# Both parts of h side by side in one tile: 512 columns at once against the high part of the weights

## Chip, cores and metric

The kernel runs on one core of one Trainium2 chip. The time is that of one execution on the device, in microseconds (us); smaller is better. The engines are TensorE (PE; its weight loads are listed apart as PEld), VectorE (DVE), ScalarE (ACT), GpSimd (POOL) and SyncE (SP, which issues the loads).

## What is computed

One encoder block on 256 tokens of 2048 channels, in float32: a normalisation, one wide input projection, two branches (latent attention, and a bidirectional RWKV-7 recurrence over 16 heads of 64), gates, a merge and an output projection.

```python
h = rms_norm(x, g_pre)                       # 256 x 2048
proj = h @ w_in                              # 2048 x 10688
mla_in, rwkv_in, z_mla, z_rwkv, gate_mla, gate_rwkv = split(proj)
y_mla  = attention(norm(q_a) @ wq_b, norm(kv_a) @ wkv_b, k_rope)
y_rwkv = groupnorm(rwkv7_bidir_scan(r, w, k, v, kk, a)) + bonus
u_mla  = (y_mla  * silu(z_mla))  @ w_br_mla
u_rwkv = (y_rwkv * silu(z_rwkv)) @ w_br_rwkv
out = (sigmoid(gate_mla) * u_mla + sigmoid(gate_rwkv) * u_rwkv) @ w_out
x = x + rms_norm(out, g_post)
```

## The kernel before, in words

**Products in three parts.** Every float32 factor is split into a high part in the faster format float32r and a low part, the rest. A product is the sum of high times high, high times low and low times high. `hhi` and `hlo` are the two parts of h, transposed: 16 blocks (k) of 128 channels by 256 tokens. The weights come in chunks of 128x1024 (`raw`): ACT casts a chunk to its high part (`whi`, L321) and DVE subtracts to get the low part (`wlo`, L324); this pair is called a split. Three chunks can be in flight.

**In-tasks.** The input projection is cut into tasks of 256 output channels (`in_task`, `cm_task`): for each of 16 k and each of two blocks of 128 channels there are three matmuls with 256 columns, L390 (whi, hhi), L391 (whi, hlo) and L392 (wlo, hhi). Both blocks add up in one PSUM bank, 256 columns each. There are 40 in-tasks: 12 for k, r, v of the recurrence (`rwkv_tasks`), 8 for z, 8 for the gates of the attention branch, 4 low-rank ones, and 8 for the gates of the RWKV branch (`gate_rwkv_task`). The first, narrow part of the projection (`LORA`) has tasks of its own. When a task's matmuls are done, its `end` reads the bank: `mix` (k, r, v), `ev_z`, a Tanh (gates) or a copy (low rank).

**Banks.** PSUM has eight banks of 512 columns: three (`DB`) hold the sums of tasks, five (`MB`) serve everything else.

**The recurrence** runs for four groups Q of four heads one after the other (`chunks_of`). Each has a *gram* stage (L791 and L799 on PE, evicted by DVE), a *solve* of small triangular systems (DVE alone: transposes L812 and L813, 60 small dependent operations, transposes L840, L842 and L844; then 32x32 matmuls L854 and L856 with copies at L861), and four *steps* along time, in each of which L886/L906/L908, a copy, L917, a copy, and L935/L938 follow on each other. After group 3 come `wkv_task` (its first matmul is L1073), `wq_task` with the attention heads, the branch products and the output projection (L1328 to L1330).

**Order.** Nothing is scheduled at run time: a planner (`Streams`) lets about twenty generators ask for an engine with a cost in us (`yield ("P", cost)`), and always takes the one that can start first, with ranks for ties; instructions are emitted in that order, engine by engine. The in-tasks' matmuls have the lowest rank on PE and fill what the recurrence leaves. So a changed cost, bank or operation can move instructions anywhere. An engine works its list strictly in order.

Of the kernel before, what the change touches and what calls it, by code (L numbers as in the profile page):

```python
# [15 lines left out]
S = 256  # L16
# [27 lines left out]
class Streams:  # L44
# [6 lines left out]
    def __init__(self):  # L51
        self.free = dict.fromkeys("PADGS", 0.0)
        self.live = []
        self.used = dict.fromkeys("PADGS", 0.0)
        self.table = None

# [20 lines left out]
    def run(self, until=None):  # L77
        while self.live and not (until and until()):
# [30 lines left out]
            if len(s[3]) > 3 and s[3][3] != self.table:  # L109
# [26 lines left out]
def cD(n):  # L136
    return 0.08 + 1.04e-3 * n
# [11 lines left out]
def encoder_block_kernel(  # L149
# [52 lines left out]
    hhi, hlo = sb([128, KT, S], "hhi", dt=F32R), sb([128, KT, S], "hlo", dt=F32R)  # L202
# [5 lines left out]
    MB = Free(pps.tile([128, 512], F32, tag=f"m{i}", bufs=1, name=f"m{i}") for i in range(5))  # L208
    DB = Free(pps.tile([128, 512], F32, tag=f"d{i}", bufs=1, name=f"d{i}") for i in range(3))
# [155 lines left out]
    def cm_task(src, nk, xhi, xlo, mt, wd, end, kc=4, load_fn=None, ready=None, kready=None, k_first=0,  # L365
                begin=None, pairs=None, first_alone=False):

        parts = []
        nb = (len(mt) + 1) // 2
# [3 lines left out]
        for i, k0 in enumerate(k0s):  # L373
# [23 lines left out]
        def take():  # L397
            b = []
            for _ in range(nb):
                b.append((yield from DB.take()))  # L400
            return b

        add_task(parts, begin or take, end, ready)
# [56 lines left out]
    def ev_second(b):  # L460
        yield ("W", lambda: len(have.get("part", ())) == 2)
        for p, m, t, B in zip(b, (96, 128), have["part"], (DB, MB)):
            yield ("D", cD(512))
            tt(w2d(t)[0:m], w2d(t)[0:m], p2(p)[0:m], ALU.add)
            B.give(p)
# [48 lines left out]
    def ev_z(b, o):  # L514

        z = p2(b[0])
        t = yield from W.take()
        yield ("A", cA(512), None, "exp")
        act.activation(w2d(t), z, AF.Tanh, scale=0.5)
        yield ("D", cD(512))  # L520
        stt(o, w2d(t), 1.0, z, ALU.add, ALU.mult)
        W.give(t)
        DB.give(*b)
# [8 lines left out]
    def gate_mla_task(g):  # L532
        def end(b):
            yield ("A", cA(512), None, "exp")
            act.activation(m16[:, 2 * g:2 * g + 2], p2(b[0]), AF.Tanh, scale=0.5)
            DB.give(*b)
        in_task(GM0 + 256 * g, end)

    def low_rank_task(c0, key):
        def end(b):  # L540
            t = yield from W.take(KEEP)
            yield ("A", cA(512))
            act.copy(w2d(t), p2(b[0]))
            DB.give(*b)
# [30 lines left out]
    def head_sums(v, m):  # L575
# [3 lines left out]
        yield ("P", 0.44)  # L579
# [1068 lines left out]
```

## Time and profile before

| | |
|---|---|
| median of 3 runs | 885.38 us (884.04 to 886.46) |
| the profiled execution | 883.63 us |
| its span, first to last instruction | 881.9 us |
| PE busy | 851.0 us, 97% |
| DVE busy | 660.1 us, 75% |
| ACT busy | 501.0 us, 57% |
| mean granted clock of TensorE | 0.984 of 2.4 GHz |

How to read it: a matmul's duration in the trace reaches from its start to a modelled end, and the next one starts long before that end. So the busy share of PE says little; what a matmul costs is the distance from one start to the next. Idle time of an engine is put down to the instruction that released it.

### The profile page before, as it was taken

Reading aid. Unit: us, or ns where it says so; the run is one execution under the profiler, and the core shown is the slowest. Engines: PE = TensorE matmul, PEld = TensorE weight load, DVE = VectorE, ACT = ScalarE, POOL = GpSimd, SP = SyncE. Lnnn points to the kernel's source line nnn. Section 1 sums busy time; section 2 is a strip of 40 time slices with the busy share of each in tenths; the row PEclk is TensorE's granted clock in tenths of the full one; section 3 lists DMA queues with packets and bytes.
Section 4 is the critical chain, followed back from the end, with each engine's and each line's share of the span. In section 5 each row is a group of like instructions: output and inputs, shape, how many; then the busy total and the mean of one; then the engine's idle time right before and its main releaser. Section 6 shows DMA issues by size and latency. Waiting matters only on the chain.

```text
span 881.9 us, 19393 instructions
## 1 busy us (share of the span) xinstructions
PE 851.0 (97%) x8112; PEld 814.6 (92%) x8112; DVE 660.1 (75%) x1082; ACT 501.0 (57%) x797; POOL 30.8 (3%) x66
## 2 busy tenths in 40 slices
PE   8999999999999999999999997979999999999996
PEld 8999999899999999999899896879999999998884
DVE  5878898867988867998868988566868556775554
ACT  6688554478444478554478543656857433444442
POOL 4110000000000000000001000000000000000000
PEclk9999999999999999999999999879999999999999
DMA  9566546534746534646525365125545675655563
GB/s 283 167 176 182 165 123 193 164 84 113 194 136 192 165 84 121 192 134 189 161 63 147 97 192 167 32 69 171 168 115 144 206 277 186 191 178 198 195 196 117
DMA packets 123528, 139.41 MB, mean 158 GB/s; under 512 B 6704, under 2 KB 110512, under 8 KB 123056
## 3 DMA queue, kind: packets, MB, share of 16 engines
q1 hardware_dynamic: 121664, 135.16, 51.9%
q0 software_dynamic: 768, 1.57, 0.6%
q8 instruction: 63, 1.03, 0.5%
q10 hardware_dynamic: 1008, 1.44, 0.5%
q14 instruction: 25, 0.20, 0.1%
HBM read 136.05 MB, written 2.10 MB: 157 GB/s over the span
## 4 chain that ended last, share of the span: by engine, by line
PE 88%; DVE 6%; ACT 3%; DMA 1%; issue 1%; POOL 0%; SPq 0%; DVEq 0%; ACTq 0%
PE d L390 19%; PE d L391 18%; PE d L392 18%; PE m L1329 2%; PE m L1330 2%; PE m L1328 2%; PE m L392 2%; PE m L391 2%; PE m L390 2%; PE m L791 2%; DVE wlo L324 2%; PE d L1329 1%; PE d L1330 1%; PE d L1328 1%; PE m L917 1%
## 5 line engine op out<-in xcount | busy, mean ns | idle before, releaser
L321 ACT CAST whi<-raw 128x1024 fp32r<-128x1024 f32 (+3 forms) x252 | 253.1, 1006 | 255.9 <-PE d L391 147.0
L324 DVE TENSOR_TENSOR wlo<-raw,whi 128x1024 fp32r<-128x1024 f32 (+3 forms) x250 | 292.3, 1170 | 121.2 <-ACT whi L321 119.3
L390 PE MATMUL d<-hhi,whi 128*128 128x256 f32 (+1 forms) x1264 | 366.4, 290 | 3.1 <-ACT u L1265 1.9
L392 PE MATMUL d<-hhi,wlo 128*128 128x256 f32 (+1 forms) x1264 | 358.5, 284 | 0.0
L391 PE MATMUL d<-hlo,whi 128*128 128x256 f32 (+1 forms) x1264 | 358.3, 283 | 0.1
L390 PEld LDWEIGHTS d<-hhi,whi 128*128 128x128 f32 (+1 forms) x1264 | 241.5, 191 | 7.6 <-ACT u L1265 2.1
L391 PEld LDWEIGHTS d<-hlo,whi 128*128 128x128 f32 (+1 forms) x1264 | 241.9, 191 | 0.4 <-DVE hlo L188 0.3
L392 PEld LDWEIGHTS d<-hhi,wlo 128*128 128x128 f32 (+1 forms) x1264 | 241.8, 191 | 0.3 <-DVE wlo L324 0.2
L185 DVE TENSOR_TENSOR work<-work,work 128x512 f32<-128x512 f32 (+5 forms) x64 | 38.9, 613 | 6.7 <-ACT work L429 4.5
L185 DVE TENSOR_TENSOR u<-u,tmp 128x30 f32<-128x30 f32 (+7 forms) x120 | 29.9, 250 | 3.1
L185 DVE TENSOR_TENSOR tmp<-u 128x30 f32<-128x30 f32 (+7 forms) x120 | 29.9, 249 | 3.0
L390 PE MATMUL d<-b,whi 128*128 128x256 f32 x96 | 27.1, 282 | 0.0
L392 PE MATMUL d<-b,wlo 128*128 128x256 f32 x96 | 27.1, 282 | 0.0
L392 PE MATMUL d<-ar,wlo 128*128 128x256 f32 x96 | 26.9, 281 | 0.0
L391 PE MATMUL d<-ar,whi 128*128 128x256 f32 x96 | 26.9, 280 | 0.0
L391 PE MATMUL d<-work,whi 128*128 128x256 f32 x96 | 26.9, 280 | 0.0
L390 PE MATMUL d<-ar,whi 128*128 128x256 f32 x96 | 26.9, 280 | 0.0
L1328 PE MATMUL m<-whi,hhi 128*128 128x512 f32 x60 | 23.3, 389 | 0.0
L1329 PE MATMUL m<-wlo,hhi 128*128 128x512 f32 x60 | 23.3, 389 | 0.0
L1330 PE MATMUL m<-whi,hlo 128*128 128x512 f32 x60 | 23.3, 389 | 0.0
L390 PE MATMUL m<-hhi,whi 128*128 128x256 f32 x80 | 23.2, 290 | 0.0
L392 PE MATMUL m<-hhi,wlo 128*128 128x256 f32 x80 | 22.6, 282 | 0.0
(335 smaller groups left out, 1536.9 us busy)
## 6 DMA issues: line engine op xcount, KB each, us to landing
raw<-in_w_in_dram SPq DMA_DIRECT2D x160, 512.0 KB, 3.9
raw<-in_w_out_dram SPq DMA_DIRECT2D x32, 512.0 KB, 3.6
raw<-in_w_br_mla_dram SPq DMA_DIRECT2D x16, 512.0 KB, 3.6
raw<-in_w_br_rwkv_dram SPq DMA_DIRECT2D x16, 512.0 KB, 3.4
raw<-in_mla_wkv_b_dram SPq DMA_DIRECT2D x8, 512.0 KB, 3.6
raw<-in_mla_wq_b_dram SPq DMA_DIRECT2D x8, 384.0 KB, 3.3
raw<-in_w_in_dram SPq DMA_DIRECT2D x7, 384.0 KB, 5.4
g<-in_x_dram SPq DMA_DIRECT2D x2, 1024.0 KB, 7.4
```

The costliest lines, as they stand in the source:

```text
L185: dve.tensor_tensor(out=o, in0=a, in1=b, op=op)
L321: act.copy(dst(c.hi), src(raw))
L324: eng.tensor_tensor(out=dst(c.lo), in0=src(raw), in1=dst(c.hi).bitcast(F32), op=ALU.subtract)
L390: pe.matmul(o, hi[:, c:c + m], xhi(k), start=k == k_first and i % 2 == 0, stop=False)
L391: pe.matmul(o, hi[:, c:c + m], xlo(k), start=False, stop=False)
L392: pe.matmul(o, lo[:, c:c + m], xhi(k), start=False, stop=last)
L791: pe.matmul(m[:, q * 128:q * 128 + 128], z.kb[R64[h], d, j, q], z.ar[d][R64[h], j, q], start=q == 0, stop=q == 3)
L917: pe.matmul(pu[R64[i], a], G[Hs, st, q, 0:64], rhs[Hs, st % 2, st // 2], start=a == 0, stop=a == 3)
L1328: pe.matmul(banks[t], hhi[:, k, T], hi, start=k == 0, stop=False)
L1329: pe.matmul(banks[t], hhi[:, k, T], lo, start=False, stop=False)
L1330: pe.matmul(banks[t], hlo[:, k, T], hi, start=False, stop=k == KT - 1)
```

## The change

`hhi` and `hlo` become the halves of one tile `hh`, so that for each k one matmul with 512 columns multiplies the high part of the weights with both parts of h, and one with 256 columns adds the low part of the weights times `hhi` to the first half. A block of 128 channels then needs a PSUM bank of its own (first half: whi·hhi + wlo·hhi; second half: whi·hlo), an in-task two banks, and `DB` has four, `MB` four. A new function `total` adds the halves at the end of a task: two ACT copies of 128x256 out of PSUM, two DVE additions of 128x256. It is used by 32 of the 40 in-tasks; the 8 of `gate_rwkv_task`, the `LORA` tasks and all later products keep their three matmuls (L409 to L411 of the changed file). In the same edit many costs given to the planner are set anew, and PE's switches between tile shapes cost 0.2 in it. What it computes is the same.

```diff
-    hhi, hlo = sb([128, KT, S], "hhi", dt=F32R), sb([128, KT, S], "hlo", dt=F32R)
+    hh = sb([128, 2, KT, S], "hh", dt=F32R)
+    hhi, hlo = hh[:, 0], hh[:, 1]
...
-    MB = Free(pps.tile([128, 512], F32, tag=f"m{i}", bufs=1, name=f"m{i}") for i in range(5))
-    DB = Free(pps.tile([128, 512], F32, tag=f"d{i}", bufs=1, name=f"d{i}") for i in range(3))
+    MB = Free(pps.tile([128, 512], F32, tag=f"m{i}", bufs=1, name=f"m{i}") for i in range(4))
+    DB = Free(pps.tile([128, 512], F32, tag=f"d{i}", bufs=1, name=f"d{i}") for i in range(4))
...
+                        if both:
+
+                            o = p2(banks[i])[0:m]
+                            pe.matmul(o, hi[:, c:c + m], both(k), start=k == k_first, stop=False)
+                            pe.matmul(o[:, 0], lo[:, c:c + m], xhi(k), start=False, stop=k == nk - 1)
+                            continue
...
-                steps.append((len(mt) * 3 * 0.109, mm) + (((lambda k=k: kready(k)),) if kready else ()))
+                steps.append((len(mt) * (0.347 if both else 3 * 0.119), mm) + (((lambda k=k: kready(k)),) if kready else ()))
...
     def in_task(c0, end, w=256, mt=PAIR, **kw):
+        kw.setdefault("both", lambda k: hh[:, :, k])
         cm_task(w_in_v[:, :, c0:c0 + w], KT, *HX, mt, w, end, **kw)
+
+    def total(b, o):
+
+        for i in range(2):
+            yield ("A", cA(256) - 0.05)
+            act.copy(o[:, i], p2(b[i])[:, 1])
+        for i in range(2):
+            yield ("D", cD(256))
+            tt(o[:, i], p2(b[i])[:, 0], o[:, i], ALU.add)
+            DB.give(b[i])
...
-                yield from mix(p2(b[0]), 128, V_MU + 8 * n + 2 * Q, w2d(t))
-                DB.give(*b)
+                yield from total(b, w2d(t))
+                yield from mix(w2d(t), 128, V_MU + 8 * n + 2 * Q, w2d(t))
...
-        yield ("D", 2.3)
+        yield ("D", 4.1)
         dve.transpose(out=Af[B1], in_=Gu[B1, :, 0:32].rearrange("p u t -> p t u"))
...
-            yield ("D", cD(n * w) + 0.02)
+            yield ("D", cD(n * w) + 0.115)
             tt(o, bc(Ai[:, j + 1:32, j:j + 1], [128, n, w]), bc(Tc[:, j:j + 1, 0:w], [128, n, w]), ALU.mult)
...
-        in_task(GR0 + 256 * g, end)
+        in_task(GR0 + 256 * g, end, both=None)
```

What stands in the engines' lists, at three places (numbers behind the names are buffers; the changed file's lines are shifted: L404 and L405 are the two new matmuls, L338 is the split L324, L191 is L185, L834 is L812).

PE, inside an in-task, one k of its two blocks. Before (`d_110` and the other d are banks):

```order
L390 MATMUL d_112<-hhi_75,whi_18_80 128x256
L391 MATMUL d_112<-hlo_76,whi_18_80 128x256
L392 MATMUL d_112<-hhi_75,wlo_21_83 128x256
L390 MATMUL d_112<-hhi_75,whi_18_80 128x256
L391 MATMUL d_112<-hlo_76,whi_18_80 128x256
L392 MATMUL d_112<-hhi_75,wlo_21_83 128x256
```

After:

```order
L404 MATMUL d_110<-hh_75,whi_17_79 128x512
L405 MATMUL d_110<-hh_75,wlo_20_82 128x256
L404 MATMUL d_111<-hh_75,whi_17_79 128x512
L405 MATMUL d_111<-hh_75,wlo_20_82 128x256
```

Six matmuls of 256 columns have become two of 512 and two of 256, in two banks. This stands 16 times in each of 32 tasks.

DVE, in the solve of group 1, the list between two splits of weights (`tmp` and `u` are the solve's small operations). Before:

```order
L324 TENSOR_TENSOR wlo_23_85<-raw_17_79,whi_20_82 128x1024
L185 TENSOR_TENSOR u_122_2980<-u_122_2980,tmp_2981 128x26x3
L185 TENSOR_TENSOR tmp_2981<-u_122_2980 128x75
L185 TENSOR_TENSOR u_122_2980<-u_122_2980,tmp_2981 128x25x3
L185 TENSOR_TENSOR tmp_2981<-u_122_2980 128x96
L324 TENSOR_TENSOR wlo_21_83<-raw_15_77,whi_18_80 128x1024
```

After (`m_43` is `m16`, where the attention branch's gates are kept):

```order
L338 TENSOR_TENSOR wlo_20_82<-raw_14_76,whi_17_79 128x1024
L191 TENSOR_TENSOR m_43_113<-d_110,m_43_113 128x256
L191 TENSOR_TENSOR u_117_2515<-u_117_2515,tmp_2516 128x26x3
L191 TENSOR_TENSOR m_43_113<-d_111,m_43_113 128x256
L191 TENSOR_TENSOR tmp_2516<-u_117_2515 128x75
L191 TENSOR_TENSOR u_117_2515<-u_117_2515,tmp_2516 128x25x3
L338 TENSOR_TENSOR wlo_21_83<-raw_15_77,whi_18_80 128x1024
```

The two additions of `total` stand among the solve's operations, and fewer of these stand between two splits. From L812 to L840 the list now has 19, 21, 22 and 19 splits in groups 0 to 3, where it had 15, 16, 15 and 15.

PE, group 3, from the last matmuls of the solve to the first step in time. Before:

```order
L886 MATMUL m_107<-uv_5640,g_198_5851 64x64 x8
L390 MATMUL d_112<-hhi_75,whi_20_82 128x256
L391 MATMUL d_112<-hlo_76,whi_20_82 128x256
L392 MATMUL d_112<-hhi_75,wlo_23_85 128x256
L390 MATMUL d_112<-hhi_75,whi_20_82 128x256
L391 MATMUL d_112<-hlo_76,whi_20_82 128x256
L392 MATMUL d_112<-hhi_75,wlo_23_85 128x256
L390 MATMUL d_112<-hhi_75,whi_20_82 128x256
L391 MATMUL d_112<-hlo_76,whi_20_82 128x256
L392 MATMUL d_112<-hhi_75,wlo_23_85 128x256
```

After (L876, L878, L908, L939, L957, L960 and L1033 are L854, L856, L886, L917, L935, L938 and L1011 of before):

```order
L876 MATMUL m_107<-u_199_5035,g_197_4973 32x32 x32
L878 MATMUL m_104<-g_197_4973,u_199_5035 32x32 x32
L908 MATMUL m_106<-uv_4892,g_197_4973 64x64 x8
L939 MATMUL m_106<-work_57_721,g_197_4973 64x64 x8
L957 MATMUL m_107<-uv_4892,b_198_4974 64x64 x8
L960 MATMUL m_105<-g_197_4973,uv_4892 64x64 x8
L908 MATMUL m_104<-uv_4896,g_197_4973 64x64 x8
L1033 MATMUL m_106<-work_31_93,ones_65 128x256
```

Before, 96 matmuls of an in-task stand between the last L854 and the first L1073; now none does. They stand ahead of the solve's matmuls, where 448 in-task matmuls follow the gram stage instead of 384.

## Rows read from the trace of the kernel before

**Rows 1.** The profile's page: span; busy us (share) and instructions of the engines.

```profile
span 881.9 us, 19393 instructions
PE 851.0 (97%) x8112; PEld 814.6 (92%) x8112; DVE 660.1 (75%) x1082; ACT 501.0 (57%) x797; POOL 30.8 (3%) x66
```

**Rows 2.** Busy us by stretch; the header names the columns, PEclk is the granted clock.

```profile
core 0: us, PE busy (x) PEld busy (x) DVE busy (x) ACT busy (x) POOL busy (x), PEclk, DMA share, GB/s
106.20:496.60 390.40, 384.31 (x4303) 370.67 (x4302) 324.14 (x543) 230.35 (x356) 11.94 (x28) 1.00 0.52 144
117.30:167.00 49.70, 49.70 (x417) 49.70 (x416) 45.38 (x91) 23.00 (x27) 0.12 (x1) 1.00 0.61 171
496.60:542.30 45.70, 45.70 (x381) 45.49 (x380) 40.72 (x89) 20.53 (x21) 0.00 (x0) 1.00 0.58 162
542.30:586.20 43.90, 30.94 (x572) 27.30 (x571) 30.37 (x52) 23.08 (x46) 0.61 (x2) 0.82 0.22 73
586.20:881.90 295.70, 287.43 (x2021) 270.22 (x2020) 184.56 (x275) 149.54 (x235) 0.00 (x0) 0.98 0.55 175
```

**Rows 3.** PE's timeline in an in-task, first and last of 28 matmuls: start, duration, instruction.

```profile
99.73 0.28 PE L391 MATMUL d<-hlo,whi 128*128 128x256 f32 x1
...
102.97 0.28 PE L391 MATMUL d<-hlo,whi 128*128 128x256 f32 x1
```

**Rows 4.** The same in the output projection, first and last of 15 matmuls.

```profile
829.74 0.39 PE L1328 MATMUL m<-whi,hhi 128*128 128x512 f32 x1
...
832.91 0.39 PE L1330 MATMUL m<-whi,hlo 128*128 128x512 f32 x1
```

**Rows 5.** Groups of DVE and ACT, 100 to 590 us: busy us, mean ns | idle.

```profile
L324 DVE TENSOR_TENSOR wlo<-raw,whi 128x1024 fp32r<-128x1024 f32 x125 | 152.9, 1223 | 27.8 <-ACT whi L321 26.9
...
L185 DVE TENSOR_TENSOR tmp<-m,z 128x256 f32<-128x256 f32 x8 | 3.4, 425 | 4.0 <-PE m L935 3.9
...
L416 ACT ACTIVATE qpad<-d,vd 128x256 f32<-128x256 f32 x18 | 8.0, 471 | 0.5 <-DVE work L185 0.4
...
L919 ACT COPY uv<-m 64x256 f32<-64x256 f32 x16 | 5.9, 366 | 1.2 <-PE m L917 0.8
```

**Rows 6.** PE's timeline of group 3, solve to `wkv_task`; in brackets idle time, releaser.

```profile
542.34 0.28 PE L392 MATMUL d<-hhi,wlo 128*128 128x256 f32 x1
544.25 0.75 PE L854 MATMUL m<-u,g 32*32 32x32 f32 x64 [1.64 <-DVE u L840]
549.44 1.07 PE L856 MATMUL m<-g,u 32*32 32x32 f32 x6 [4.43 <-DVE g L844]
550.65 1.05 PE L856 MATMUL m<-g,u 32*32 32x32 f32 x58 [0.15 <-DVE u L861]
...
578.04 0.23 PE L908 MATMUL m<-ar,z 64*64 64x64 f32 x2
580.03 0.68 PE L917 MATMUL m<-work,g 64*64 64x64 f32 x16 [1.76 <-DVE work L912]
581.54 1.16 PE L938 MATMUL m<-g,uv 128*64 128x64 f32 x16 [0.84 <-ACT uv L919]
584.61 0.58 PE L581 MATMUL m<-work,bdr 128*128 128x256 f32 x1 [1.91 <-ACT work L429]
...
586.15 0.41 PE L1073 MATMUL d<-b,whi 128*128 128x256 f32 x1
```

**Rows 7.** One step of group 3 in the same timeline.

```profile
561.23 0.69 PE L935 MATMUL m<-uv,b 128*64 128x64 f32 x16
561.75 0.64 PE L938 MATMUL m<-g,uv 128*64 128x64 f32 x16
...
562.78 0.27 PE L906 MATMUL m<-z,ar 64*64 64x64 f32 x2
...
563.25 0.23 PE L908 MATMUL m<-ar,z 64*64 64x64 f32 x2
```

**Rows 8.** PE's waits over the whole span: us in total, times, longest.

```profile
PE m L856 <- DVE g L844: 4.4, 1, 4.4
PE m L856 <- DVE u L861: 3.1, 7, 1.1
```

More of the change, by code (lines that the diff above doesn't have):

```diff
@@ L108, in run @@
             e, cost = s[3][0], s[3][1]
-            if len(s[3]) > 3 and s[3][3] != self.table:
+            if e == "P":
+                mode = s[3][3] if len(s[3]) > 3 else "128x128"
+                cost += 0.2 * (mode != self.mode)
+                self.mode = mode
+            elif len(s[3]) > 3 and s[3][3] != self.table:
                 self.table = s[3][3]
@@ L207, in encoder_block_kernel, with take_banks @@
     W = Free(works[:-1])
-    MB = Free(pps.tile([128, 512], F32, tag=f"m{i}", bufs=1, name=f"m{i}") for i in range(5))
-    DB = Free(pps.tile([128, 512], F32, tag=f"d{i}", bufs=1, name=f"d{i}") for i in range(3))
+    MB = Free(pps.tile([128, 512], F32, tag=f"m{i}", bufs=1, name=f"m{i}") for i in range(4))
+    DB = Free(pps.tile([128, 512], F32, tag=f"d{i}", bufs=1, name=f"d{i}") for i in range(4))
+    def take_banks(n):
+        b = []
+        for _ in range(n):
+            b.append((yield from DB.take()))
+        return b
     yr = sb([128, 8, 256], "yr")
@@ L365, in cm_task @@
     def cm_task(src, nk, xhi, xlo, mt, wd, end, kc=4, load_fn=None, ready=None, kready=None, k_first=0,
-                begin=None, pairs=None, first_alone=False):
+                pairs=None, first_alone=False, both=None):
         parts = []
-        nb = (len(mt) + 1) // 2
         k0s = list(range(k_first, nk, kc))
@@ L392, in mm @@
                         pe.matmul(o, lo[:, c:c + m], xhi(k), start=False, stop=last)
-                steps.append((len(mt) * 3 * 0.109, mm) + (((lambda k=k: kready(k)),) if kready else ()))
+                steps.append((len(mt) * (0.347 if both else 3 * 0.119), mm) + (((lambda k=k: kready(k)),) if kready else ()))
             parts.append((load, list(pairs(k0, kc)) if pairs else plain(kc * wd), steps))
[L397 to L403, printed above, removed]
+        add_task(parts, lambda: take_banks(len(mt) if both else (len(mt) + 1) // 2), end, ready)
     HX = (lambda k: hhi[:, k]), (lambda k: hlo[:, k])
@@ L514, in ev_z @@
     def ev_z(b, o):
-        z = p2(b[0])
+        yield from total(b, o)
         t = yield from W.take()
         yield ("A", cA(512), None, "exp")
-        act.activation(w2d(t), z, AF.Tanh, scale=0.5)
+        act.activation(w2d(t), o, AF.Tanh, scale=0.5)
         yield ("D", cD(512))
-        stt(o, w2d(t), 1.0, z, ALU.add, ALU.mult)
+        stt(o, w2d(t), 1.0, o, ALU.add, ALU.mult)
         W.give(t)
-        DB.give(*b)
     def z_task(c0, key):
@@ L533, in end @@
         def end(b):
+            o = m16[:, 2 * g:2 * g + 2]
+            yield from total(b, o)
             yield ("A", cA(512), None, "exp")
-            act.activation(m16[:, 2 * g:2 * g + 2], p2(b[0]), AF.Tanh, scale=0.5)
-            DB.give(*b)
+            act.activation(o, o, AF.Tanh, scale=0.5)
         in_task(GM0 + 256 * g, end)
@@ L541, in end @@
             t = yield from W.take(KEEP)
-            yield ("A", cA(512))
-            act.copy(w2d(t), p2(b[0]))
-            DB.give(*b)
+            yield from total(b, w2d(t))
             have[key] = t
@@ L928, in chunks_of @@
             cost = 1.0 if q < 3 else 0.5
-            e = yield ("P", 0.2 + cost + (0.5 if q < 3 else 0.0), eu)
+            e = yield ("P", cost + (0.5 if q < 3 else 0.0), eu, "128x64")
             if q < 3:
@@ L1055, in begin @@
                     tt(t[R64[i]], kr[R64[i]], att["kr"][0][R64[i]].bitcast(F32), ALU.subtract)
-            a = yield from DB.take()
-            b = yield from DB.take()
-            return a, b
+            return (yield from take_banks(2))
         parts = []
@@ L1098, in wq_task @@
         wq_v = wq_b.rearrange("(k p) (h c) -> p k h c", p=128, c=192)
-        def begin():
-            a = yield from DB.take()
-            b = yield from DB.take()
-            return a, b
         parts = []
@@ L1150, in end @@
                 O.add(head(g, i), 1, O.free["D"])
-        add_task(parts, begin, end, lambda: have["qhl"][1] if "qhl" in have else None)
+        add_task(parts, lambda: take_banks(2), end, lambda: have["qhl"][1] if "qhl" in have else None)
     def half_split(src, hi, lo, n):
@@ L1313, in begin @@
                 MB.tiles.clear()
-            a = yield from DB.take()
-            b = yield from DB.take()
-            return a, b
+            return (yield from take_banks(2))
         parts, more = [], []
@@ L1332, in out_task @@
                 for t in range(2):
-                    steps[t if n == 3 and k0 >= 6 else 0].append((3 * 0.216, lambda b, hi, lo, mm=mm, t=t: mm(b, hi, lo, t)))
+                    steps[t if n == 3 and k0 >= 6 else 0].append((3 * 0.227, lambda b, hi, lo, mm=mm, t=t: mm(b, hi, lo, t)))
             pairs = [(512, lambda t, i=i: half(t, i), lambda t, i=i: half(t, i)) for i in range(2)]
@@ L1517, in pairs_first @@
                ("kr", 0 if k0 < 2 else 2 if k0 < 8 else 8))
-    def begin_second():
-        a = yield from DB.take()
-        b = yield from MB.take()
-        return a, b
     LORA = [(0, 96), (128, 96), (256, 128), (384, 128)]
```

54 lines of the change are left out of this document (27 added, 27 removed).

## Prediction

> **What bounds the kernel now.** The page comes first: PE is busy for 97% of the span, DVE for 75%, ACT for 57% [rows 1]. Since a matmul's modelled duration overlaps the next one's, 97% alone proves little, so the next view is PE's timeline inside an in-task, read from start to start. 28 matmuls of 256 columns follow each other without a gap from 99.73 to 102.97 us, 27 steps of 0.120 us [rows 3]. PE issues there as fast as it does anywhere, and every 0.120 us taken out of such a stretch is gained, if nothing else becomes late. The busy times by stretch say where that holds. From the eviction of group 0's gram stage to the solve of group 3, 106.2 to 496.6 us, PE is busy 384.3 of 390.4 us at full granted clock, and DVE 324.1, 83% [rows 2]. In the solve of group 0 (117.3 to 167.0) DVE is busy 45.4 of 49.7 us, 91%: the second engine is close behind. From 586.2 us to the end PE is busy again, 287.4 of 295.7 us. The one place where PE is not the limit is between these two, 542.3 to 586.2 us: PE busy 30.9 of 43.9 us, mean granted clock 0.82 [rows 2]. There the last in-tasks run out, and the recurrence of group 3 has to end before `wkv_task` may begin. PE's timeline shows that chain: L854 waits for a transpose, L856 4.43 us for another, L917 1.76 us for a copy, L938 0.84 us, L581 1.91 us, and L1073 starts at 586.15 [rows 6].
>
> So a gain made in the in-tasks has to pass through this place: what counts is by how much L1073 comes earlier.
>
> **The change, part by part.**
>
> *The matmuls.* Per k and block, three matmuls of 256 columns (3 x 0.120 = 0.360 us) become one of 512 and one of 256. For 512 columns the output projection has the row: 15 matmuls from 829.74 to 832.91, 14 steps of 0.226 us [rows 4]. The pair costs 0.346, so 0.0136 us is saved: two starts of 256 columns cost 0.240, one of 512 columns 0.226. 32 tasks x 16 k x 2 blocks = 1024 pairs, 13.9 us in all. The bounds: nothing, if a 256 behind a 512 costs more than one behind another 256 (no row shows this alternation), and 13.9. I take 13.9: the 512 of the row is also the same array, format and weight load, its moving operand alone lies elsewhere.
>
> [...]
>
> *Additions and copies.* `total` puts 64 DVE additions of 128x256 with one operand in PSUM into the lists. The nearest row, the same operation on the same shape with an operand from PSUM, has 0.425 us [rows 5]: 27.2 us. 64 ACT copies out of PSUM cost between 0.366 (a plain copy of 256 columns) and 0.471 us (with a scale) [rows 5]: 23 to 30 us. Four copies of the low-rank tasks go. ACT was busy 57% [rows 1] and would come to some 60%: nothing on the path, since each copy has a whole task (32 x 0.346 = 11.1 us) before its bank is wanted again: two tasks fit into four banks. On DVE the price is nothing as long as it fits beside PE. From 106.2 to 496.6 us some 20 of the 32 tasks end, 20 x 2 x 0.425 = 17 us: 324 + 17 = 341 us, while PE's time there shrinks by 20 x 32 x 0.0136 = 8.7 to 381.7 us. That is 89%, less than the 91% at which PE did not wait from 117.3 to 167.0. If the cover were gone, up to 27 us would lie on the path. I take 0 and keep the 27 for a rival.
>
> *Order.* Two things move. In each solve DVE now meets 19 to 22 splits where there were 15 or 16, so more in-task work lies beside a solve, and about four instead of five of its small operations stand between two splits. At 2.77 us for a chunk (8 x 0.346) 19 splits last 53 us; DVE needs for them 19 x 1.22 [rows 5] = 23 us beside the solve itself, so the solve is paced by PE, as before. And in group 3 the 96 in-task matmuls that stood between the steps in time (96 x 0.120 = 11.5 us) now stand ahead of L854. PE's list before that L854 is then about as long in time as it was: what the pairs save there is filled by what moved there. I therefore let PE reach it at 542 us again, and the question is how long the chain takes without its fillers.
>
> One step, bare: from the end of L908 to L917 1.76 us (578.27 to 580.03), L917 to L938 1.51 [rows 6], L935 to L906 1.55, L906 to the end of L908 0.70 (562.78 to 563.48) [rows 7]: 5.5 us, three times 16.6. The last L917 to the end of L938 is 2.67, from there to L1073 3.45 (582.70 to 586.15) [rows 6]. Before them, from L854 to the first L917, no bare row exists. At least L854 0.75, a copy of some 1.3 with its way there and back, L856 2.26 (549.44 to 551.70), again 1.3, the first L886 at about 0.95 and 1.76 to L917: 8.3 us; at most the time between L854 and its first L917 now, under 15 us. I take 11, because four Tanh of gates now queue on ACT ahead of the first copy. Sum 33.7 us, with 31 to 38 as bounds, against 43.8 from 542.34 to 586.15. A thinner PE is also likelier to be granted half the clock here: L938 took 1.16 us where it took 0.64 elsewhere [rows 6, 7]; half a microsecond for each of some four groups more is 2 us. So L1073 comes 8.1 us earlier by this place, 3.4 less than the 11.5 us of matmuls that left it.
>
> *Costs and banks.* Four instead of five `MB` banks can hold up gram matmuls until DVE has evicted; new costs for transposes and small operations can take away waits such as L856 for L861, 3.1 us in seven times [rows 8]. Either is worth 0 to about 3 us, with opposite signs: I take 0 for both. After L1073 the same work follows, unchanged.
>
> *The sum.* -13.9 (pairs) + 3.4 (of the 11.5 us moved out of the exposed place, what comes back as waiting) = -10.5 us. The profiled execution, 883.6 us with a span of 881.9, becomes 873.1; its time is 1.8 us under the median of 885.4, so the median becomes 874.9: 875.
>
> **The rivals.**
>
> *The matmuls save nothing.* If what a matmul costs beyond its columns is tied to the columns or to the bank instead of to the instruction, the pair stays at 0.360. For it: no row alternates the two sizes. Against it: 0.226 is less than twice 0.120 [rows 3, 4]. Then only the return of 3.4 us is left, or nothing: 885 to 889. [...]
>
> *DVE sets the pace (slower).* The mechanism: DVE works in order, and an addition that waits for an ACT copy, or merely stands ahead of a split, makes the next `wlo` late; PE waits for it with the whole in-task. The place is the solves and the gram stages of groups 0 to 2. In the solve of group 0 DVE has 45.4 us of work in 49.7 [rows 2]; 4.3 tasks of 96 x 0.120 = 11.5 us end in that time, 3.7 us of additions, 49.1 us, while PE would need only 49.7 - 4.3 x 32 x 0.0136 = 47.8. It decides from there on: where DVE's work exceeds PE's, the difference is lost. With half of the 27 us exposed the time is 875 + 13.6 = 889, with all of it 902. Against it: the list spreads the solve over more splits, so that fewer of its operations go with each.
>
> *The recurrence of group 3 gives all of it back.* If the bare chain takes as long as the filled one, L1073 stays at 586, 8.1 us of the gain are lost: 883. For it: five waits of the chain are there already [rows 6]. Against: fillers and splits now stand between its links, and a step's own parts add to 5.5 us.
>
> *More than the sum.* If the truer costs take the waits at L856 away (3.1 us) and nothing comes back at group 3 (3.4 us), the time is 868.
>
> **How the numbers follow.** The forecast, 870 to 881, has a chance of 0.56; more than the sum (864 to 870) 0.12; all given back at group 3 (881 to 886) 0.13; no saving by the matmuls 0.07; DVE sets the pace 0.12. The measurement of this kernel can tell about 0.3%, 2.7 us, from no change: faster is below 882.7, slower above 888.0. Faster: 0.56 + 0.12 + 0.08 of the third = 0.76; same: 0.05 of the third, most of the fourth, some 0.01 of the last: 0.12; slower: 0.12. A range of 865 to 886 leaves out DVE's case, a part of the fourth and the lowest end, under 2 in 10.
>
> **What would show it.** In the changed profile: starts of L404 and L405 0.226 and 0.120 us apart (if it is 0.36 for the pair, the first step is wrong); DVE busy about 85 to 92% from group 0's gram to group 3's solve and no wait of L405 for L338 above a few us in total (else DVE sets the pace); the last L854 at 535 to 545 us and the first matmul of `wkv_task` 31 to 38 us behind it, near 578; from there 295 us to the end. The prediction is wrong if L404 waits for banks (`total` too late), if the in-tasks run out before the solve of group 3 has ended, or if the changed order moves other work behind L1073.

## The result and the profile after

The changed kernel takes 913.3 us (median of 4 runs, 912.7 to 914.3) against 885.3 us before: a ratio of 1.0317, 95% interval 1.0300 to 1.0335. It is 28 us slower where 10 us less were forecast. The page of the profiled execution, the lines that answer to [rows 1]:

```profile
span 911.9 us, 17486 instructions
PE 857.0 (94%) x7088; PEld 766.4 (84%) x7088; DVE 679.8 (75%) x1146; ACT 516.8 (57%) x855; POOL 29.9 (3%) x66
```

1024 matmuls are gone, PE is busy for 6 us more, and the span is 30.0 us longer. The busy times by stretch, cut at the events that matter (columns as in [rows 2]): group 0's gram stage, the end of group 2's recurrence, the end of the gap that follows, the last in-task, the first matmul of `wkv_task`, the end.

```profile
107.70:478.90 371.20, 362.10 (x3338) 309.58 (x3337) 318.12 (x561) 225.00 (x367) 12.18 (x28) 1.00 0.53 147
478.90:518.00 39.10, 23.35 (x140) 18.60 (x140) 25.16 (x36) 19.16 (x36) 0.64 (x2) 0.64 0.15 40
518.00:578.40 60.40, 60.38 (x452) 58.44 (x452) 43.79 (x97) 24.54 (x28) 0.00 (x0) 0.95 0.55 157
578.40:617.40 39.00, 21.95 (x475) 17.67 (x474) 25.77 (x48) 18.07 (x41) 0.61 (x2) 0.68 0.09 28
617.40:911.90 294.50, 286.40 (x2022) 268.89 (x2020) 184.83 (x275) 148.41 (x234) 0.00 (x0) 0.99 0.57 176
```

Read the second and fourth line first. In each PE is busy for little more than half of 39 us, at 0.64 and 0.68 of its clock, with DMA nearly still. Before, only the second of these places existed, 43.9 us at 0.82 [rows 2]. Where the first one lies now, from the end of group 2 (465.3 us) to the gram stage and on to the solve's matmuls, PE was busy for 21.4 of 21.4 and 54.1 of 57.6 us, at full clock:

```profile
465.30:486.70 21.40, 21.40 (x190) 21.07 (x190) 17.25 (x22) 18.52 (x33) 1.10 (x3) 1.00 0.51 144
486.70:544.30 57.60, 54.06 (x473) 52.36 (x475) 52.56 (x107) 26.95 (x31) 0.00 (x0) 1.00 0.55 152
```

From the first matmul of `wkv_task` to the end nothing changed: 294.5 us, 295.7 before [rows 2]. So all 30 us are lost ahead of it: it starts at 617.4 and not at 586.2 [rows 6].

PE's timeline at the first of the two places:

```profile
482.45 0.28 PE L405 MATMUL d<-hh,wlo 128*128 128x256 f32 x1
482.57 0.38 PE L664 MATMUL m<-iv,work 128*128 128x128 f32 x2
...
493.42 2.08 PE L813 MATMUL m<-ar,u 64*128 64x128 f32 x16
...
501.63 2.07 PE L813 MATMUL m<-ar,u 64*128 64x128 f32 x14 [4.62 <-ACT b L800]
...
511.23 1.11 PE L821 MATMUL m<-iv,u 128*128 128x128 f32 x4
518.02 0.79 PE L404 MATMUL d<-hh,whi 128*128 128x512 f32 x1 [5.67 <-DVE work L191]
518.61 0.41 PE L405 MATMUL d<-hh,wlo 128*128 128x256 f32 x1
```

Between 482.6 and 518.0 us no in-task matmul stands in PE's list. What runs is group 3's own front (the operations ahead of its gram stage) and gram stage, bare, for the most part at half the clock (granted 0.5, which is 1.2 of 2.4 GHz, from 486.4 to 496.6 and from 500.0 to 523.9; 16 gram matmuls take 2.08 us). The first in-task behind it waits 5.67 us for its bank, until the late sums of a low-rank task (`work` L191) have run. Behind that wait stands the solve of group 3. On DVE it reaches from the first transpose L834 to L862, 65.1 us; before, the same two (L812 and L840) stood 45.6 us apart. Before, then after:

```profile
496.59 2.02 DVE L812 STREAM_TRANSPOSE u<-g 32x1024 f32<-32x1024 f32 x1
542.17 2.03 DVE L840 STREAM_TRANSPOSE u<-u 32x1024 f32<-32x1024 f32 x1
```

```profile
513.12 1.89 DVE L834 STREAM_TRANSPOSE u<-g 32x1024 f32<-32x1024 f32 x1
...
517.55 0.42 DVE L191 TENSOR_TENSOR work<-d,work 128x256 f32<-128x256 f32 x1
...
578.22 2.02 DVE L862 STREAM_TRANSPOSE u<-u 32x1024 f32<-32x1024 f32 x1
```

The second place, to be held against [rows 6]:

```profile
578.39 0.28 PE L411 MATMUL d<-hh,wlo 128*128 128x256 f32 x1
580.30 0.75 PE L876 MATMUL m<-u,g 32*32 32x32 f32 x64 [1.63 <-DVE u L862]
585.49 1.06 PE L878 MATMUL m<-g,u 32*32 32x32 f32 x6 [4.43 <-DVE g L866]
...
592.00 1.12 PE L939 MATMUL m<-work,g 64*64 64x64 f32 x16 [2.57 <-DVE work L934]
...
617.42 0.42 PE L1092 MATMUL d<-b,whi 128*128 128x256 f32 x1
```

The in-tasks end at 578.4 us, before the solve's matmuls, and group 3's recurrence runs without any. And the pair itself, in an in-task of the changed kernel:

```profile
130.16 0.40 PE L404 MATMUL d<-hh,whi 128*128 128x512 f32 x1
130.39 0.28 PE L405 MATMUL d<-hh,wlo 128*128 128x256 f32 x1
...
132.99 0.40 PE L404 MATMUL d<-hh,whi 128*128 128x512 f32 x1
```

Eight pairs from 130.16 to 132.99: 0.354 us each, where the triple had 0.360 [rows 3]. Counted over all 884 pairs ahead of `wkv_task` that another pair follows directly at full clock (less than 0.4 us from start to start), the mean is 0.350 us.

### The profile page after: what moved, and what is told of

It reads as the page before. It is cut to its first block, busy times and chain, and to the rows that moved or that the text cites. A ratio compares the mean times of both kernels' runs of the same rounds, so it can differ in the third digit from the quotient of the medians.

```text
span 911.9 us, 17486 instructions
## 1 busy us (share of the span) xinstructions
PE 857.0 (94%) x7088; PEld 766.4 (84%) x7088; DVE 679.8 (75%) x1146; ACT 516.8 (57%) x855; POOL 29.9 (3%) x66
## 4 chain that ended last, share of the span: by engine, by line
PE 76%; DVE 13%; ACT 7%; issue 2%; DMA 1%; POOL 0%; SPq 0%; DVEq 0%; ACTq 0%
PE d L404 20%; PE d L405 10%; PE d L409 7%; PE d L411 7%; PE d L410 7%; DVE wlo L338 3%; DVE work L191 2%; PE m L813 2%; PE m L1340 2%; PE m L1341 2%; PE m L1342 2%; PE d L1340 2%; PE d L1341 2%; PE d L1342 2%; ACT whi L335 1%
## 5 line engine op out<-in xcount | busy, mean ns | idle before, releaser
L338 DVE TENSOR_TENSOR wlo<-raw,whi 128x1024 fp32r<-128x1024 f32 (+3 forms) x250 | 292.2, 1170 | 130.5 <-ACT whi L335 129.1
L404 PE MATMUL d<-hh,whi 128*128 128x512 f32 x1024 | 370.2, 403 | 5.7 <-DVE work L191 5.7
L405 PE MATMUL d<-hh,wlo 128*128 128x256 f32 x1024 | 288.9, 282 | 2.5 <-DVE wlo L338 2.5
L404 PEld LDWEIGHTS d<-hh,whi 128*128 128x128 f32 x1024 | 193.4, 189 | 51.3 <-DVE work L191 6.3
L405 PEld LDWEIGHTS d<-hh,wlo 128*128 128x128 f32 x1024 | 195.2, 191 | 3.2 <-DVE wlo L338 3.2
L409 PE MATMUL d<-hh,whi 128*128 128x256 f32 (+1 forms) x320 | 91.4, 286 | 0.0
L411 PE MATMUL d<-hh,wlo 128*128 128x256 f32 (+1 forms) x320 | 90.5, 283 | 0.0
L410 PE MATMUL d<-hh,whi 128*128 128x256 f32 (+1 forms) x320 | 90.4, 282 | 0.0
L409 PEld LDWEIGHTS d<-hh,whi 128*128 128x128 f32 (+1 forms) x320 | 60.3, 189 | 0.1
L410 PEld LDWEIGHTS d<-hh,whi 128*128 128x128 f32 (+1 forms) x320 | 60.4, 189 | 0.1
L411 PEld LDWEIGHTS d<-hh,wlo 128*128 128x128 f32 (+1 forms) x320 | 60.3, 189 | 0.0
L191 DVE TENSOR_TENSOR work<-work,work 128x512 f32<-128x512 f32 (+5 forms) x64 | 39.0, 613 | 11.6 <-ACT work L453 4.5
L409 PE MATMUL d<-b,whi 128*128 128x256 f32 x128 | 36.2, 283 | 0.0
L411 PE MATMUL d<-b,wlo 128*128 128x256 f32 x128 | 36.2, 282 | 0.0
L411 PE MATMUL d<-ar,wlo 128*128 128x256 f32 x128 | 36.0, 281 | 0.0
L410 PE MATMUL d<-ar,whi 128*128 128x256 f32 x128 | 35.9, 281 | 0.0
L409 PE MATMUL d<-ar,whi 128*128 128x256 f32 x128 | 35.8, 280 | 0.0
L191 DVE TENSOR_TENSOR u<-u,tmp 128x30 f32<-128x30 f32 (+7 forms) x120 | 29.9, 249 | 2.6
L191 DVE TENSOR_TENSOR tmp<-u 128x30 f32<-128x30 f32 (+7 forms) x120 | 29.7, 248 | 2.4
L813 PE MATMUL m<-ar,u 64*128 64x128 f32 x256 | 24.4, 324 | 6.1 <-ACT b L800 6.0
```

The lines of the kernel that those rows point to most:

```text
L191: dve.tensor_tensor(out=o, in0=a, in1=b, op=op)
L338: eng.tensor_tensor(out=dst(c.lo), in0=src(raw), in1=dst(c.hi).bitcast(F32), op=ALU.subtract)
L404: pe.matmul(o, hi[:, c:c + m], both(k), start=k == k_first, stop=False)
L405: pe.matmul(o[:, 0], lo[:, c:c + m], xhi(k), start=False, stop=k == nk - 1)
L409: pe.matmul(o, hi[:, c:c + m], xhi(k), start=k == k_first and i % 2 == 0, stop=False)
L410: pe.matmul(o, hi[:, c:c + m], xlo(k), start=False, stop=False)
```

## Experiments

The theories, numbered as the expectations name them. **1:** two banks for each task leave two tasks in flight instead of three, and when both wait to be emptied PE has nothing beside group 3. **2:** the new planner costs moved the fillers. **3:** the sums slow VectorE. **4:** the pairs save nothing; the pairs just counted answer it, they save 0.010 us each. **5** came after the first four runs. A *block* is one k of 128 output channels, a pair or a triple of matmuls; 1216 of them precede `wkv_task`. In the table, "done" is how many have started when group 2's recurrence ends (its last matmul on L939, or on the same line under another number), "left" how many follow up to `wkv_task`, both counted in the trace; then the times of the two events, the median and the ratio to the kernel before with its interval.

| kernel | done / left | group 2 ends | wkv starts | median us | ratio |
|---|---|---|---|---|---|
| before | 1009 / 207 | 465.3 | 586.1 | 885.3 | |
| changed | 1049 / 167 | 478.9 | 617.4 | 913.3 | 1.0317 (1.0300-1.0335) |
| e1 costs alone | 933 / 283 | 446.6 | 577.3 | 873.0 | 0.9882 (0.9867-0.9897) |
| e2 before, two banks | 1009 / 207 | 481.0 | 615.1 | 922.4 | 1.0424 (1.0393-1.0454) |
| e3 one bank held | 1049 / 167 | 478.4 | 607.9 | 904.6 | 1.0238 (1.0222-1.0253) |
| e4 former costs | 1018 / 198 | 463.4 | 580.4 | 878.8 | 0.9946 (0.9929-0.9964) |
| e5 pair counted 0.38 | 947 / 269 | 457.4 | 589.8 | 883.1 | 0.9986 (0.9970-1.0003) |
| e6 e1, two banks | 933 / 283 | 454.7 | 585.2 | 892.0 | 1.0082 (1.0063-1.0100) |
| e7 two more gates | 1049 / 231 | 479.8 | 630.7 | 918.2 | 1.0388 (1.0365-1.0411) |
| e8 sums uncounted | 973 / 243 | 457.5 | 584.7 | 881.6 | 0.9966 (0.9948-0.9983) |
| e9 sums left out | 1049 / 167 | 473.4 | 606.2 | 904.3 | 1.0220 (1.0191-1.0249) |
| e10 e5, sums left out | 947 / 269 | 449.7 | 580.4 | 875.2 | 0.9892 (0.9868-0.9916) |
| e11 e5, keep one | 951 / 265 | 456.5 | 583.6 | 878.9 | 0.9929 (0.9905-0.9952) |
| e12 e8, keep one | 973 / 243 | 462.7 | 594.9 | 890.9 | 1.0069 (1.0045-1.0092) |
| e13 keep one | 1049 / 167 | 478.5 | 605.7 | 902.5 | 1.0208 (1.0191-1.0225) |
| e14 splits on GpSimd | 947 / 269 | 469.9 | 603.2 | 898.1 | 1.0157 (1.0135-1.0179) |
| e15 e1, solve counted long | 1037 / 179 | 481.5 | 604.9 | 902.0 | 1.0208 (1.0177-1.0239) |

**e1: the new costs alone.** The kernel before with the diff's cost lines and nothing else, such as:

```diff
-                steps.append((len(mt) * 3 * 0.109, mm) + ...
+                steps.append((len(mt) * 3 * 0.119, mm) + ...
...
-            yield ("D", cD(n * w) + 0.02)
+            yield ("D", cD(n * w) + 0.115)
```

> The kernel before, with nothing of the change but the new planner costs and the 0.2 us that the planner adds where PE's kind of matmul changes; banks (five and three), triples of 256 columns and the end of each task stay. Theory 1 (two banks for each in-task leave two tasks in flight where there were three, and none is left beside group 3's front and gram): the costs alone do no harm, 870 to 888 us, with in-task matmuls in every stretch up to group 3's solve. Theory 2 (the new costs moved the fillers away from group 3): 900 us or more, with the same empty stretch of some 30 us at 483 to 518 us that the changed kernel shows.

Measured: 873.0 us, 1.2% faster than before and the lowest median of all. Theory 2 falls as it stood.

```profile
101.50:446.60 345.10, 336.63 (x3870) 322.41 (x3869) 291.47 (x505) 201.55 (x313) 12.33 (x29) 1.00 0.50 140
446.60:578.10 131.50, 129.47 (x1451) 124.84 (x1452) 108.24 (x185) 79.00 (x120) 1.13 (x3) 1.00 0.50 141
578.10:870.80 292.70, 284.28 (x2012) 266.68 (x2010) 184.28 (x274) 146.34 (x231) 0.00 (x0) 0.99 0.56 180
```

From the end of group 2 to `wkv_task` PE is busy for 129.5 of 131.5 us at full clock: neither gap exists. 283 blocks were left for this stretch.

**e2: the kernel before, with two banks for tasks.**

```diff
-    DB = Free(... for i in range(3))
+    DB = Free(... for i in range(2))
```

> The kernel before with two banks in place of three for the tasks, so that two are in flight as in the changed kernel, and nothing else: no pairs, no added halves, the former costs. Theory 1 (tasks in flight): 895 to 910 us, with a stretch of more than 20 us around group 3's gram in which PE has no in-task matmul and its granted clock falls to 0.5. Theory 2 (costs) and theory 3 (the added copies and sums make the splits late): 885 us, within 3 us.

Measured: 922.4 us, beyond theory 1's range, with the same counts as before. Its trace has the changed kernel's picture: no in-task for 23.4 us from 489.5 us on, and a solve of group 3 of 57.3 us. Losing a task in flight can cost that much in the former order; whether it is what costs in the changed kernel is not told by it.

**e3: one bank held.** The low-rank tasks add their halves into their first bank and give the second back before they wait for the work tile they keep (they take it when six others are free besides).

```diff
+            u = yield from W.take()
...
+                tt(o[:, i], p2(b[i])[:, 0], uv_[:, i], ALU.add)
+            DB.give(b[1])
+            W.give(u)
             t = yield from W.take(KEEP)
-            yield from total(b, w2d(t))
+            act.copy(w2d(t), o)
+            DB.give(b[0])
```

> The changed kernel, where the four low-rank tasks add their halves into their first bank and give the second one back before they wait for the work tile that they keep, so that a waiting one holds one bank and not two. One more transient tile and one more 128x512 copy for each of four tasks. Theory 1 (waiting tasks hold all four banks): the empty stretch before group 3's solve shrinks, 890 to 900 us. Theories 2 and 3 (costs; the added work on VectorE): as the changed kernel, 913 us, within 3 us.

Measured: 904.6 us; 8.7 of the 28 us come back, less than theory 1 asked for.

**e4: the changed kernel with the former costs**, the same lines the other way; for a pair:

```diff
-                steps.append((len(mt) * (0.347 if both else 3 * 0.119), mm) + ...
+                steps.append((len(mt) * (0.327 if both else 3 * 0.109), mm) + ...
```

> The changed kernel with the former planner costs (a pair at 0.327 us, which is three times 0.109), and without the costs' knowledge of PE's kinds of matmul; banks, pairs and sums stay as changed. Theory 1 (tasks in flight): still 900 us or more, with a stretch of over 20 us without in-task matmuls beside group 3. Theory 2 (the new costs moved the fillers): 885 us or less.

Measured: 878.8 us. Theory 1 falls in its simple form: two banks for a task, two tasks in flight, and faster than before. Costs alone gain, pairs alone gain, both together lose 28 us. The blocks told why. The planner runs in-task blocks beside each group's solve for as long as it believes the solve to take. Counted in the traces from the first gram matmul to the first L856 in groups 0 to 2: 158 to 162 blocks before, 182 to 196 with the new costs (longer solve), 174 to 196 with pairs and sums (the sums stand in DVE's queue too), 206 to 220 with both. So theory **5**: the order spends the blocks on groups 0 to 2, and too few are left for group 3, whose chain has a length of its own.

**e5: the changed kernel, a pair counted 0.38.** Nothing else.

```diff
-                steps.append((len(mt) * (0.347 if both else 3 * 0.119), mm) + ...
+                steps.append((len(mt) * (0.38 if both else 3 * 0.119), mm) + ...
```

> The changed kernel with one number altered: the planner counts 0.38 us for a pair of matmuls and not 0.347, so that it sets fewer in-task blocks of 128 channels beside each group. By the end of group 2's recurrence 946 of the 1216 blocks stand in PE's list, where the changed kernel has 1048, the one with the former costs 1018 and the one with the new costs alone 932. Banks, pairs, copies and sums stay. New theory 5 (the order spends the in-tasks on groups 0 to 2, and what is left is shorter than group 3's chain): PE has work up to the first matmul of wkv, near 575 us, and the total is 865 to 880 us. Theory 1 (two tasks in flight starve group 3): 900 us or more. Theory 3 (VectorE's added work slows each group): 885 to 900 us, with PE waiting for splits.

Measured: 883.1 us: 30.2 us come back, all that was lost (the ratio's interval reaches 1), by one number that only sets the order. It is 3 us above theory 5's range; e10 shows a cost of the sums that is larger than that.

**e6: e1 with two banks for tasks**, the edit of e2 on the kernel of e1.

> The kernel before with the new planner costs and two banks for tasks in place of three, without pairs, copies and sums: two tasks in flight, and by the end of group 2's recurrence 932 of 1216 blocks in PE's list, as with three banks. Theory 1 (tasks in flight): 895 us or more. Theory 5 (blocks left for group 3): 873 to 880 us, since as many are left as with three banks.

Measured: 892.0 us, in neither range, near theory 1's number, but not for its reason:

```profile
109.50:454.70 345.20, 336.75 (x3870) 322.47 (x3869) 291.81 (x506) 201.62 (x313) 12.33 (x29) 1.00 0.51 140
454.70:585.90 131.20, 129.55 (x1451) 124.85 (x1452) 107.97 (x185) 79.01 (x120) 1.13 (x3) 1.00 0.50 141
585.90:890.00 304.10, 288.24 (x2012) 270.11 (x2010) 184.54 (x274) 146.51 (x231) 0.00 (x0) 0.98 0.54 173
```

Line by line against e1: 345.2 and 345.1 us, 131.2 and 131.5. The two banks cost 8.0 us ahead of group 0's gram and 11.4 us behind `wkv_task`, whose tasks take two banks each, and nothing where the changed kernel loses its time.

**e7: two more gate tasks ahead of `wkv_task`.**

```diff
-GPRE, MIX = 4, [0, 1, 1, 1]
+GPRE, MIX = 6, [0, 1, 1, 0]
```

> The changed kernel with six gate tasks of 32 blocks ahead of wkv in place of four; the other two stay between the wq tasks. Up to group 2's recurrence nothing changes (1048 blocks); 40 more blocks of triples, some 14 us of PE work, stand between that and the end of group 3's recurrence. Theory 5 (too little work left beside group 3's chain): first wkv matmul within 3 us of the 617.4 us of before this edit less nothing, but 64 blocks fewer behind it, 890 to 900 us. Theory 1 (tasks in flight alone, in the stretch of group 3's gram): 908 to 915 us, since that stretch stays as it is.

Measured: 918.2 us; theory 5 had forecast 890 to 900 and was wrong here. `wkv_task` starts 13.3 us later for 64 more blocks, which are 23 us of triples, so the gap did take some 10 us of work. But the same gates were the cover of the attention heads:

```profile
631.50:700.00 68.50, 68.15 (x561) 67.18 (x561) 49.82 (x103) 46.61 (x94) 0.00 (x0) 1.00 0.53 155
700.00:735.00 35.00, 26.37 (x158) 23.84 (x157) 19.68 (x48) 17.51 (x43) 0.00 (x0) 0.80 0.26 86
```

Between 700 and 735 us PE now has 26.4 us of work at 0.80 of the clock. The gap had moved.

**e8: the sums uncounted.** In `total`:

```diff
-            yield ("D", cD(256))
+            yield ("D", 0.01)
             tt(o[:, i], p2(b[i])[:, 0], o[:, i], ALU.add)
```

> The changed kernel, where the planner counts the two sums of each task at 0.01 us each; they run as before on VectorE, 0.42 us each. Only the order changes: 972 blocks by the end of group 2's recurrence in place of 1048. Theory 5 (order): 868 to 885 us. Theory 3 (VectorE cannot carry the sums): 895 us or more, with PE waiting for splits and for banks. Theory 1: 900 us or more.

Measured: 881.6 us. Every instruction of the changed kernel runs, in another order, and 31.7 us are back.

**e9: the sums left out** of the changed kernel, order kept. The expectation's "56 us" is a slip; its second figure, 27 us, holds.

```diff
-            act.copy(o[:, i], p2(b[i])[:, 1])
+            act.copy(o[:, i], p2(b[i])[:, 0])
...
-            tt(o[:, i], p2(b[i])[:, 0], o[:, i], ALU.add)
```

> The changed kernel in its own order, with the two sums of each in-task left out: the copies take the products of the high and the low part of the weights with the high part of h, and the products with the low part of h are computed and never added. VectorE has 56 us less queued; in fact 64 sums of 0.42 us, 27 us, fall away. Theory 3 (VectorE's added work slows the groups): 885 to 895 us. Theory 5 (the order has spent the blocks): 908 to 914 us, since the 1048 blocks still stand ahead of the end of group 2's recurrence.

Measured: 904.3 us, between the two. The sums cost 9.0 us; the other 19 remain.

**e10: e5 with the sums left out**, both edits together.

> The changed kernel with 0.38 us counted for a pair, as in the run of 883.1 us, and with the sums left out in the same way. The order stays as in that run, so that it shows what the sums cost VectorE where PE has work all along. Theory 3: 870 to 876 us, which would explain the 10 us between that run and the new costs alone. If the sums are hidden: 881 to 884 us.

Measured: 875.2 us, 7.9 less than e5. So the sums cost 8 to 9 us in either order. With them gone and the pairs kept, e10 is no faster than e1, which has neither (the intervals overlap): the order of these two differs, and where the pairs' own saving went between them is open.

**e11 and e12: e5 and e8, where the low-rank tasks wait for less.**

```diff
-            t = yield from W.take(KEEP)
+            t = yield from W.take(1)
             yield from total(b, w2d(t))
             have[key] = t
```

> The changed kernel with 0.38 us counted for a pair, and with the four low-rank tasks content with one work tile left free in place of six when they take the tile that they keep, so that they give their two banks back at once. No stretch without in-task blocks is left ahead of wkv in the order. If the banks held by waiting tasks explain what is left (PE at 0.5 of its clock at 425 to 436 and 473 to 477 us in the run of 883.1 us): 872 to 878 us. If not: 881 to 885 us.

> The changed kernel, where the planner counts the two sums of a task at 0.01 us each (the run of 881.6 us) and the four low-rank tasks are content with one work tile left free. Meant to beat both kernels: 868 to 876 us if the banks held by waiting tasks are what is left beside the order; 880 to 883 us if not.

Measured: 878.9 us, 4 less than e5 and just above the range for the banks; and 890.9 us, 9 more than e8. The second contradicts both of its forecasts. Its counts at group 2's end are e8's; it falls behind in small steps, 5 us up to there and 5 more in group 3's solve. What causes them is open.

**e13: the edit of e11 alone, in the changed kernel.**

> The changed kernel, where the four low-rank tasks are content with one work tile left free in place of six and so give their banks back at once; costs, sums and pairs as changed, and 1048 blocks by the end of group 2's recurrence as there. If the banks held by waiting tasks are the cause: 880 to 887 us. If too few blocks are left for group 3: 897 to 908 us, with a stretch of over 25 us without in-task blocks beside group 3's recurrence.

Measured: 902.5 us, in the range for too few blocks. The waiting tasks are worth 10.8 us, and theory 5's stretch is there:

```profile
478.50:561.50 83.00, 76.74 (x591) 71.46 (x592) 66.85 (x121) 42.81 (x63) 0.64 (x2) 0.94 0.48 134
561.50:607.00 45.50, 25.91 (x482) 21.45 (x481) 28.59 (x60) 19.00 (x43) 0.61 (x2) 0.58 0.09 25
```

The first gap is nearly closed, 76.7 of 83.0 us; the second has grown to 45.5 us at 0.58 of the clock.

**e14: pairs at 0.365 us, every sixth split on GpSimd**, to make the pairs pay.

```diff
-WLG = [2, 4]
+WLG = [2, 4] + list(range(20, 150, 6))
...
-                on, eng, cost = ("G", gp, 1.85) if i in WLG else ("D", dve, cD(n))
+                on, eng, cost = ("G", gp, 1.85 if i < 9 else 2.6) if i in WLG else ("D", dve, cD(n))
```

> The changed kernel with 0.365 us counted for a pair, and with every sixth split of a chunk after the twentieth on GpSimd in place of VectorE, 22 in all; 27 us of VectorE's work go to an engine that is busy for 30 of 912 us. In the order 946 of 1216 blocks stand ahead of the end of group 2's recurrence, and no in-task is missing up to wkv. If order and VectorE's load are the two causes: 866 to 874 us, below both kernels. If GpSimd's slower splits make PE wait: 880 us or more.

Measured: 898.1 us, inside the forecast for late splits, but in the trace PE waits for splits only 2.1 us in all, 0.7 of it for GpSimd's. GpSimd's splits made VectorE slower:

```profile
L191 DVE TENSOR_TENSOR u<-u,tmp 128x30 f32<-128x30 f32 (+7 forms) x120 | 38.4, 320 | 2.8
L191 DVE TENSOR_TENSOR tmp<-u 128x30 f32<-128x30 f32 (+7 forms) x120 | 38.3, 320 | 2.8
```

The solve's small operations take 320 ns in the mean, 249 in the changed kernel. The timeline shows one of the eight that make the mean:

```profile
138.48 2.40 POOL L338 TENSOR_TENSOR wlo<-raw,whi 128x1024 fp32r<-128x1024 f32 x1 [23.30 <-ACT whi L335]
138.61 2.38 DVE L191 TENSOR_TENSOR u<-u,tmp 128x96 f32<-128x96 f32 x1
```

The small operation lasts as long as the split that started 0.13 us ahead of it.

**e15: the order, without the change.** e1 (triples, three banks, no sums), each of the solve's 60 steps counted 0.125 us longer.

```diff
-            yield ("D", cD(n * w) + 0.115)
+            yield ("D", cD(n * w) + 0.24)
```

> The kernel of the run with the new costs alone (873.0 us: triples, three banks for tasks, no sums), where the planner counts each of the 60 steps of a group's solve 0.125 us longer than there. Nothing that runs changes but the order: 1036 of 1216 blocks by the end of group 2's recurrence in place of 932. Theory 5 (too few blocks left for group 3): 893 to 908 us, with a stretch of over 20 us without in-task blocks ahead of wkv. If banks, pairs or sums of the change are needed for the loss: 872 to 880 us.

Measured: 902.0 us, 29 us more than e1. Only the order differs. PE at group 3's solve:

```profile
549.14 0.28 PE L398 MATMUL d<-hhi,wlo 128*128 128x256 f32 x1
562.92 1.08 PE L860 MATMUL m<-u,g 32*32 32x32 f32 x64 [13.51 <-DVE u L846]
```

The in-tasks that stand ahead of the solve's matmuls end (32 blocks stand behind), and PE waits 13.5 us for the solve. Against e1, 104 blocks more stand ahead of group 2's end, which comes 34.9 us later, and the stretch from there to `wkv_task`, with 104 blocks fewer, is only 7.4 us shorter. A wrong number in the planner, without the change's banks, pairs and sums, makes a loss of the same size.

## Why the prediction failed

**The failed step is the order.** The prediction said: "PE's list before that L854 is then about as long in time as it was [...] I therefore let PE reach it at 542 us again." The list was about as long (1024 pairs at 0.350 us and 192 triples at 0.360, 428 us; 1184 triples before, 426), but PE reached that line (now L876) at 580.3 us and not at 544.25 [rows 6]. A sum up to one instruction does not see where in it the work stands. By the traces, 13.6 of these 36 us are lost up to the end of group 2, 2.9 from there to L834, and 19.5 in group 3's solve.

*Ahead of group 2's end.* Group 3's recurrence needs group 2's final state, and from the end of group 2 to `wkv_task` no run here took less than 117 us, whatever lay beside it (the table's two times; e4 is the lowest). Up to the end of group 2 PE is nearly full, 362 of 371 us, so a block set there delays that end; behind it, blocks are cheap as long as they fit beside the chain. e15 against e1 shows it: 0.34 us later for each block moved ahead. The changed order moved 40 blocks that way, and 167 are left for a stretch that holds 283 in e1; the sums make 5.5 of the 13.6 us (e9). The count is no full measure. In e5, 102 blocks fewer than in the changed kernel bring group 2's end only 21.5 us forward, and e4 with 1018 blocks done is faster than e5 with 947.

*Behind it.* The stretch to `wkv_task` is not at its shortest either, 138.5 us where it was 120.9. Seven of the 167 blocks follow group 2's end at once; then none lies beside group 3's front and gram stage, and the other 160 stand between that and L876, where 128 stood. They begin at 518.0 us, and from there to 578.4 PE is full: the solve, whose operations stand among their splits, goes at the pace of PE. Where the low-rank tasks give their banks back sooner, 124 (e3) and 122 (e13) of the blocks stand there, and the solve lasts 46.3 and 47.0 us. The prediction had the figure in hand: "19 splits last 53 us" is 7 us more than the 45.7 of [rows 2], and it was not carried into the path.

e8 and e5 (order alone, -32 and -30 us) and e15 (order alone, +29) show from both sides that the order makes the loss. How much of it is the number of blocks ahead of group 2's end, and how much their place behind it, is split by the traces and not by a run of its own. Of the signs named in advance, "L404 waits for banks" came true (5.67 us); that the in-tasks end before the solve tells nothing, since L876 waits 1.63 us there and L854 waited 1.64 [rows 6].

**The new costs, a term put at nothing.** The prediction had them worth "0 to about 3 us" by waits such as that of L856, and took 0. It did not ask what else they would move. They are worth a gain of 1.2%, some 11 us, in the kernel before (e1) and a loss of some 34 us in the changed one (913.3 against e4's 878.8). Four banks instead of five for everything else, the other half of that term, has no run of its own; e4, e5 and e8 have four and reach 878.8 to 883.1 us, so the loss is not made by them alone.

**The banks: a step that was wrong as a cost of nothing.** The prediction's "two tasks fit into four banks" left out that four low-rank tasks hold theirs until, besides the work tile they take, six are free. In the changed order they meet group 3's front, which uses those tiles. e3 and e13 price it: 8.7 and 10.8 of the 28 us by the medians, 7 and 10 by the ratios. This overlaps with the order and is not added to it. It is a price in this order alone: the same edit as e13's gains 4 us on e5 (e11) and loses 9 on e8 (e12), which stays unexplained.

**Additions costed at nothing, mis-sized:** 8 to 9 us (e9, e10). The rival "DVE sets the pace" had a true core, but no wait of L405 for splits shows it: from 107 to 482 us these come to 2.5 us. In e9's trace 5.5 us are gained by the end of group 2 and 5.7 from there to `wkv_task`. The planner's count of these same sums, which lengthens each group in its eyes, is what e8 took away.

**Pairs, mis-sized:** 0.350 us in the mean and not 0.346, some 10 us in 1024 pairs instead of 13.9, inside the bounds named. The doubt about the untried alternation of sizes was right to be there.

**Group 3's chain, mis-sized:** last in-task to `wkv_task` 39.0 us, forecast 35.7, with waits at the places named. The forecast's "542 us again" and "near 578" also leave out 2.4 us of its own sum (13.9 saved less 11.5 moved in), a slip that changes nothing here. **Held:** full speed of PE in the in-tasks up to the end of group 2, and 294.5 us from `wkv_task` to the end.

## To carry to other kernels

Where a serial chain runs beside a pool of filler work, find the last event the chain cannot pass early, and count in the new order how much filler stands before it and how much behind: only the second lies beside the chain. A planner's cost that is long for the chain, or short for the filler, spends filler early, and the true cost is not always the safe one: 0.347 us for a pair was nearly right, and 0.38 gave 30 us back. Two edits that each gain can lose together, so time them apart (the costs alone are the version to keep here: 873.0 us). A buffer doubled per task leaves fewer tasks in flight, here two instead of three, which is to be checked against the task that holds it longest.

## What the hardware showed unexpectedly

A matmul of 512 columns was followed by the one of 256 after 230 to 241 ns, most often 230, where 512 followed by 512 took 226 [rows 4]; the 256 by the next 512 after 113 to 120 ns (both in the in-tasks at full clock).

In e14, 8 of the 240 small operations of the solves took 2.3 to 2.5 us where the longest had been 0.3, each begun 0.05 to 0.3 us behind the start of a GpSimd split of 2.4 to 2.5 us. The mean rose by 71 ns, over 240 operations 17 us. The Trainium skill ("SBUF — State Buffer", section "SBUF: two separate sides") says that VectorE and GpSimd share a pair of ports as an exclusive lock held for the whole instruction, also against a VectorE operation with two inputs in SBUF. By that rule the trace agrees: 2.38 us behind 2.40.
